# A hybrid decoder block on one core: the second projection unit of the first half in plain products instead of Strassen-Winograd products

## The chip, the cores and the metric

The kernel runs on one core of a Trainium2 chip. The metric is the device time of one execution in microseconds; the time of a kernel is the median of its runs. The core's engines work side by side, each on its own queue of instructions in a fixed order: TensorE (PE, matrix products into PSUM), VectorE (DVE), ScalarE (ACT), GpSimd (POOL), and SyncE (SP), which here issues all DMA transfers. An instruction that waits holds up what stands behind it on its engine.

## The reference

The block takes 2048 tokens of width 1024: a normalised input goes through one projection to two mixers (gated linear attention in chunks, and a short gated convolution), their outputs through one output projection, and then through a SwiGLU feed-forward part.

```python
h = rmsnorm(x, norm1_g[l])
proj = h @ w_in[l]
p_q, p_k, p_v, p_g, p_a, c_b, c_c, c_h = jnp.split(proj, splits, axis=-1)
...
log_a = (jax.nn.log_sigmoid(p_a @ w_gate_up[l] + b_gate[l]) / GATE_NORMALIZER)
o = gla_chunked(q, k, v, log_a)
o = rmsnorm(o, gla_norm_g[l]) * jax.nn.silu(p_g)
o_conv = c_b * causal_depthwise_conv(c_c * c_h, conv_w[l])
x = x + jnp.concatenate([o_gla, o_conv], axis=-1) @ w_out[l]
x = x + (jax.nn.silu(h2 @ w_ffn_gate[l]) * (h2 @ w_ffn_up[l])) @ w_ffn_down[l]
return rmsnorm(x, norm_f_g)
```

## The kernel before

**Precision.** Every float32 operand of a product is held as two parts, a high one that ACT rounds off and a low one that DVE gets by subtraction (`split`, L146 and L147). One step of a product (`product_step`, L334 to L336) is three matmuls of 128x128 by 128x512: high by high, high by low, low by high.

**Tiling.** Activations are transposed: features on the partitions, tokens along the row, in tiles of 128x512 (`h`). The 2048 tokens go in two halves of 1024, each half in two column blocks j = 0 and 1. The normalised input of a half is a 2x2 matrix of blocks B11 (features 0 to 511, j = 0), B12 (the same, j = 1), B21 and B22 (features 512 to 1023), each of four tiles k.

**Units.** The columns of a weight matrix are taken in units of 256, a 2x2 matrix of quarters A11, A12, A21, A22. `unit` computes a unit's four output tiles (r, j) with seven products instead of eight (the Winograd form of Strassen's method, `PRODUCTS`): A11 B11, S1 T1, S2 T2, A12 B21, S3 T3, S4 B22, A22 T4. The S are sums and differences of weight quarters, which POOL makes (L317, L318, L319, L324). The T are differences of activation blocks: T1 = B12 - B11, T2 = B22 - T1, T3 = B22 - B12, T4 = B21 - T2. A product is four steps, twelve matmuls. The outputs come out of sums of products: ACT copies a bank of PSUM (L354), PE adds a further product to the same bank, which must wait for the copy, and DVE adds the bank to a copy (L358). Split weights go into four buffers (`wq`), raw weights into two (`raw`), split activations (`op`) into 28.

**The first half's start.** `build_first` (L259) scales the tiles by the norm (DVE, L460), splits them, and computes unit 0 (the first 256 columns, the keys) beside that in eight plain products straight from the B blocks (L283 to L285), since the T don't exist yet. It then has POOL make the sixteen tiles of T1 to T4 (L294; each is written over one of the `h` tiles: T1, T2 and T4 over those of B11, T3 over those of B12) and splits them. Unit 1 (the queries) and all later units go through `unit` with the T. B12 itself has no further reader after unit 0, and its buffers go to later `op` tiles.

**Projections of a half.** `in_proj` (L556) takes twelve units: keys, queries, two of values, two of the output gate with silu (units 4 and 5), and six for the convolution. A step of other work is put in after each product (`tick`, L187): a list `background` of generators, of which one step is taken at every tick while `hurry` is set, later at every second. The list for the first half is `gate_weights`, a number of empty steps (`pause(6)`, L995), `row_stats(2)` and `row_stats(3)` (squares of the second half's rows on ACT, L412), `gate(0, ops)` (the forget gate: sixteen and twenty-four small-weight products into a_ps, L517, then exp, ln and scans, L538 to L551, and stores to s_d), and `h1_ahead`, the second half's B and T ahead of their use (L460, L240 to L253 and splits named hi and lo). The gate uses exp and ln, the output gate uses silu; ACT must load a table when it changes between them.

**Order.** The calls above give the program's order; a scheduler with its own time model then moves instructions on each engine's queue as dependencies allow. At run time each queue is taken in order.

Of the kernel before, what the change touches and what calls it, by code (L numbers as in the profile page):

```python
# [14 lines left out]
ALU = mybir.AluOpType  # L15
# [32 lines left out]
def tile_hymba_block(ctx, tc, x, xt, win, wa, wgu, wout, wffn, wdown, wdown_first, small, out):  # L48
# [149 lines left out]
    def pause(n):  # L198
        for _ in range(n):
            yield  # L200
# [6 lines left out]
    def split_op(src):  # L207
        o = opp.tile([P, 2, PB], F32R, name="op", tag="op")
        split(src, o[:, 0, :], o[:, 1, :])
        return o  # L210
# [48 lines left out]
    def build_first(quad, w):  # L259


        ops = {b: [] for _, b in PRODUCTS}
        h, o = {}, {}
        quarters = ("A11", "A12"), ("A21", "A22")
        los = []
        for j in range(2):
            for r in range(2):
                o[r, j] = bank()
            for k in range(KD):
                with ExitStack() as stack:  # L270
                    if len(los) > 1:
                        stack.enter_context(tc.issue_after(los[-2].ins))
                    h[k, j] = quad(k, j)
                x = opp.tile([P, 2, PB], F32R, name="op", tag="op")
                los.append(split(h[k, j][:], x[:, 0, :], x[:, 1, :]))
                if j == 0 and k >= PT:
                    row_squares(1, k - PT)
                name = ("B11", "B12")[j] if k < 4 else ("B21", "B22")[j]
                ops.setdefault(name, []).append(x)
                c = slice(k % 4 * P, (k % 4 + 1) * P)  # L280
                for r in range(2):
                    q = w[quarters[r][k // 4]]
                    pe.matmul(o[r, j][:], q[:, 0, c], x[:, 0, :], start=k == 0, stop=False)  # L283
                    pe.matmul(o[r, j][:], q[:, 0, c], x[:, 1, :], start=False, stop=False)
                    pe.matmul(o[r, j][:], q[:, 1, c], x[:, 0, :], start=False, stop=k == KD - 1)  # L285
            if j == 0:
                rbs[1] = rows_rstd(squares[1])
        for n, y, a, b in (
            ("T1", (0, 0), (0, 1), (0, 0)), ("T2", (0, 0), (4, 1), (0, 0)),
            ("T3", (0, 1), (4, 1), (0, 1)), ("T4", (0, 0), (4, 0), (0, 0)),  # L290
        ):
            for k in range(4):
                yy, aa, bb = [h[k + dk, j] for dk, j in (y, a, b)]
                pool.tensor_tensor(yy[:], aa[:], bb[:], ALU.subtract)  # L294
                ops[n].append(split_op(yy[:]))
        return ops, [(r, j, o[r, j], True) for j in range(2) for r in range(2)]

    def weight_quarter(src):
        n = src.shape[-1]
# [38 lines left out]
    def unit(src, ops, into=None):  # L338


        w = unit_weights(src)

        def mul(i, o=None):
            first = o is None
            o = bank() if first else o
            n, m = PRODUCTS[i]
            for k in range(len(ops[m])):
                product_step(o, w[n], ops[m], k, first)
            tick()
            return o  # L350

        def copied(name, o, at):
            t = tt(name) if into is None else into[at]
            act.activation(t[:], o[:], AF.Copy)  # L354
            return t

        def plus(t, o):
            dve.tensor_tensor(t[:], o[:], t[:], ALU.add)  # L358
            return t


        oa = mul(0)
        c11 = copied("c11", oa, (0, 0))
        ob = mul(1)
        c22 = copied("c22", ob, (1, 1))
        mul(2, oa)
        c12 = copied("c12", oa, (0, 1))
        plus(c11, mul(3))
        mul(4, oa)
        plus(c22, oa)  # L370
        mul(5, ob)
        plus(c12, ob)
        mul(6, oa)
        if into is not None:
            copied("c21", oa, (1, 0))
        return [(0, 0, c11, False), (1, 1, c22, False), (0, 1, c12, False), (1, 0, oa, True)]
# [176 lines left out]
            yield  # L553
        decays[b] = em, dn, el

    def in_proj(half, ops, first):  # L556
        def units():
            for u in range(12):
                with ExitStack() as stack:
                    if half == 0 and u == 1:  # L560
                        stack.enter_context(tc.issue_after(last_load[0].ins))
                    yield first if u == 0 and first else unit(win[u], ops)

        units = units()
        for dst, i0 in ((s_kq, 0), (s_kq, 2), (s_v, 0), (s_v, 2)):
            for r, j, c, p in next(units):
                store(dst[2 * half + j][i0 + r][:], settled(c, p)[:])
        for i0 in (0, 2):
            for r, j, c, p in next(units):
                store(s_g[2 * half + j][i0 + r][:], silu(c, p)[:])  # L570
        background.append(gla_half(half))
        for i0 in (0, 2):
            cc = {(r, j): settled(c, p) for r, j, c, p in next(units)}
            ch = {(r, j): c for r, j, c, _ in next(units)}
            for r in range(2):
                i = i0 + r
                for j in range(2):
                    s = tp.tile([P, PB + 2], F32, name="u", tag="t")
                    dve.tensor_tensor(s[:, 2:], ch[r, j][:], cc[r, j][:], ALU.mult)
                    dve.tensor_copy(s[:, 0:2], halo[:, i, :])  # L580
                    dve.tensor_copy(halo[:, i, :], s[:, PB : PB + 2])
                    y = cc[r, j]
                    dve.tensor_scalar(y[:], s[:, 0:PB], col(C_CW + i), None, ALU.mult)
                    for n in (1, 2):
                        dve.scalar_tensor_tensor(
                            y[:], s[:, n : n + PB], col(C_CW + 4 * n + i), y[:], ALU.mult, ALU.add
                        )
            for r, j, c, _ in next(units):
                y = cc[r, j]
                dve.tensor_tensor(y[:], c[:], y[:], ALU.mult)  # L590
                hi = tp.tile([P, PB], F32R, name="hi", tag="t")
                split(y[:], hi[:], y[:].bitcast(F32R))
                dst = s_mix[2 * half + j][i0 + r]
                store(dst[:, 0, :], hi[:].bitcast(F32))
                store(dst[:, 1, :], y[:])
# [338 lines left out]
    def last_unit(src, ops, b12, y, ssq):  # L934
# [49 lines left out]
        for j in range(2):  # L984
# [3 lines left out]
    act.preload_act_table_set("natural_log_exp_and_others")  # L988
    first_loads()
    load(wgu_sb[:], wgu)  # L990
    ops, first = build_h()
    hurry.append(True)
    background.extend(
        [
            gate_weights(), pause(6), row_stats(2), row_stats(3), gate(0, ops), unhurried(),  # L995
            h1_ahead(),
        ]
    )
    in_proj(0, ops, first)
    drain_background(lambda: len(background) < 2)  # L1000
    ops = load_pairs(s_h1)
    background.append(gate(1, ops))
    in_proj(1, ops, None)
    drain_background(lambda: (1, PT - 1) in done)
    ssq = out_proj(0, build_mix(0))
    drain_background(lambda: (3, PT - 1) in done)
# [117 lines left out]
```

## Time and profile before

| what | value |
| --- | --- |
| runs | 2144.77, 2137.0, 2141.64 us; median 2141.64 |
| profiled execution | 2147.18 us, its span 2145.4 us |
| PE busy | 2052.6 us, 96% of the span |
| DVE, ACT, POOL busy | 1438.1, 1008.4, 983.5 us |
| mean granted clock of PE | 0.983 |

The profile shows one execution. A page gives the busy time of each engine and the groups of instructions; the timeline gives instructions in order of time (start, duration, engine, line, operation, what is written and read, and in brackets the idle time before it and what ended that); the table of waits gives, for each pair of waiting and releasing line, the time in total, how often, and the longest. Matmul durations overlap, since one enters the array while the one before drains: what a matmul costs is the distance between two starts. Where a row shows an instruction many times (x6), its duration spans them all. Line numbers are those of the kernel before.

### The profile page before, as it was taken

What the parts mean: (1) busy time and instruction counts of PE and PEld (TensorE: products, weight loads), DVE (VectorE), ACT (ScalarE), POOL (GpSimd) and SP (SyncE); (2) the same over time, 40 slices, a digit from 0 to 9 for tenths busy, and PEclk for the clock granted to TensorE, in tenths of its full rate; (3) what the DMA queues carried; (4) which work ended last, traced back from release to release, by engine and by line L of the source; (5) the groups of instructions that cost most, each with busy time, mean ns of one, the idle gap of its engine ahead of it and who ended that gap; (6) DMA issues with size and microseconds to landing.
All of it is one profiled execution on the core that took longest, in us unless ns stands there. A gap on an engine that the chain in (4) does not pass through costs nothing.

```text
span 2145.4 us, 26958 instructions
## 1 busy us (share of the span) xinstructions
PE 2052.6 (96%) x9137; PEld 1658.6 (77%) x9137; DVE 1438.1 (67%) x2035; ACT 1008.4 (47%) x1961; POOL 983.5 (46%) x707
## 2 busy tenths in 40 slices
PE   6899899999999999999999999999999999999996
PEld 4677787887788887788888887787888888887774
DVE  7668975548664496688887674654686677664554
ACT  6455345564544334554555453333464454553344
POOL 3425422221201374555655436774644654435773
PEclk9899999999999999999999999999999999999998
DMA  7348667432486982466454577688455455587662
GB/s 270 125 145 296 225 267 249 154 121 88 154 305 190 348 295 103 167 246 220 181 226 177 208 303 266 257 333 351 155 199 210 148 188 196 186 334 275 265 265 108
DMA packets 191563, 471.85 MB, mean 220 GB/s; under 512 B 20032, under 2 KB 65344, under 8 KB 181824
## 3 DMA queue, kind: packets, MB, share of 16 engines
q1 hardware_dynamic: 191424, 470.12, 60.5%
q8 instruction: 72, 1.18, 0.2%
q14 instruction: 67, 0.55, 0.1%
HBM read 301.22 MB, written 168.82 MB: 219 GB/s over the span
## 4 chain that ended last, share of the span: by engine, by line
PE 73%; DMA 10%; DVE 10%; issue 3%; ACT 3%; POOL 1%; SPq 0%; DVEq 0%; ACTq 0%; POOLq 0%
PE mm L334 21%; PE mm L336 21%; PE mm L335 21%; DVE wq L147 2%; PE mm L742 2%; PE mm L745 2%; PE mm L743 2%; DMA raw<-in_wdown_dram 1%; DVE op L147 1%; DMA op<-sa_B 1%; DVE h L460 1%; DMA op<-shT 1%; DMA raw<-in_wffn_dram 1%; PE a_ps L517 1%; DVE so L147 1%
## 5 line engine op out<-in xcount | busy, mean ns | idle before, releaser
L334 PE MATMUL mm<-op,wq 128*128 128x512 f32 x2495 | 987.4, 398 | 31.1 <-ACT c L354 17.0
L336 PE MATMUL mm<-op,wq 128*128 128x512 f32 x2495 | 971.7, 394 | 19.6 <-DVE wq L147 18.8
L335 PE MATMUL mm<-op,wq 128*128 128x512 f32 x2495 | 979.0, 392 | 2.6 <-DVE op L147 2.6
L147 DVE TENSOR_TENSOR wq<-raw,wq 128x512 fp32r<-128x512 f32 (+2 forms) x628 | 532.2, 852 | 306.7 <-ACT wq L146 304.9
L146 ACT ACTIVATE wq<-raw 128x512 fp32r<-128x512 f32 (+2 forms) x628 | 367.7, 589 | 582.1 <-PE mm L336 416.0
L334 PEld LDWEIGHTS mm<-op,wq 128*128 128x128 f32 x2495 | 473.2, 190 | 151.2 <-ACT c L354 22.9
L336 PEld LDWEIGHTS mm<-op,wq 128*128 128x128 f32 x2495 | 473.1, 190 | 129.9 <-DVE wq L147 30.4
L335 PEld LDWEIGHTS mm<-op,wq 128*128 128x128 f32 x2495 | 473.9, 190 | 102.2 <-DVE op L147 4.3
L319 POOL TENSOR_TENSOR raw<-s,raw 128x512 f32<-128x512 f32 (+2 forms) x98 | 130.8, 1335 | 439.2 <-DVE wq L147 391.2
L358 DVE TENSOR_TENSOR c<-mm,c 128x512 f32<-128x512 f32 x270 | 185.3, 686 | 121.7 <-PE mm L336 119.6
L317 POOL TENSOR_TENSOR s<-raw 128x512 f32<-128x512 f32 (+2 forms) x98 | 128.5, 1311 | 196.5 <-DMA raw<-in_wffn_dram 92.2
L324 POOL TENSOR_TENSOR raw<-raw 128x512 f32<-128x512 f32 (+2 forms) x98 | 128.6, 1313 | 144.6 <-DVE wq L147 119.5
L354 ACT ACTIVATE c<-mm 128x512 f32<-128x512 f32 x270 | 156.6, 586 | 27.6 <-PE mm L336 27.0
L724 POOL TENSOR_TENSOR ssx<-ssx,q 128x512 f32<-128x512 f32 x52 | 74.6, 1447 | 152.8 <-ACT q L723 152.7
L318 POOL TENSOR_TENSOR raw<-raw 128x512 f32<-128x512 f32 (+2 forms) x98 | 138.5, 1414 | 4.5
L904 POOL TENSOR_TENSOR y<-c,y 128x512 f32<-128x512 f32 x66 | 99.3, 1506 | 68.4 <-DVE c L358 68.2
L146 ACT ACTIVATE wq<-s 128x512 fp32r<-128x512 f32 (+2 forms) x98 | 57.7, 589 | 103.3 <-PE mm L336 101.1
L147 DVE TENSOR_TENSOR so<-t,so 128x512 fp32r<-128x512 f32 x100 | 89.5, 902 | 23.5 <-ACT so L146 23.4
L742 PE MATMUL mm<-op,wq 128*128 128x512 f32 x256 | 100.7, 394 | 0.0
L743 PE MATMUL mm<-op,wq 128*128 128x512 f32 x256 | 99.8, 390 | 0.0
L147 DVE TENSOR_TENSOR wq<-s,wq 128x512 fp32r<-128x512 f32 (+2 forms) x98 | 87.0, 888 | 15.7 <-ACT wq L146 15.1
L146 ACT ACTIVATE so<-t 128x512 fp32r<-128x512 f32 x100 | 62.7, 629 | 48.4 <-DMA sa_B<-so 22.5
(173 smaller groups left out, 1893.1 us busy)
## 6 DMA issues: line engine op xcount, KB each, us to landing
raw<-in_wffn_dram SPq DMA_DIRECT2D x44, 1024.0 KB, 5.9
sa_T<-so SPq DMA_DIRECT2D x88, 512.0 KB, 4.6
op<-sa_T SPq DMA_DIRECT2D x88, 512.0 KB, 9.6
sa_B<-so SPq DMA_DIRECT2D x69, 512.0 KB, 3.4
op<-sa_B SPq DMA_DIRECT2D x69, 512.0 KB, 9.5
raw<-in_win_dram SPq DMA_DIRECT2D x23, 1024.0 KB, 5.7
raw<-in_wdown_dram SPq DMA_DIRECT2D x24, 768.0 KB, 6.2
sx<-y SPq DMA_DIRECT2D x48, 256.0 KB, 4.8
```

Source lines behind the costliest of these rows:

```text
L146: last_hi[:] = [act.activation(hi, src, AF.Copy)]
L147: return dve.tensor_tensor(lo, src, hi.bitcast(F32), ALU.subtract)
L318: pool.tensor_tensor(a21, a11, a21, ALU.subtract)
L319: pool.tensor_tensor(a11, s1, a11, ALU.subtract)
L324: pool.tensor_tensor(a12, a12, a11, ALU.subtract)
L334: pe.matmul(o[:], wh, xh, start=first and k == 0, stop=False, skip_group_check=True)
L335: pe.matmul(o[:], wh, xl, start=False, stop=False, skip_group_check=True)
L336: return pe.matmul(o[:], wl, xh, start=False, stop=k == n - 1, skip_group_check=True)
L354: act.activation(t[:], o[:], AF.Copy)
L358: dve.tensor_tensor(t[:], o[:], t[:], ALU.add)
L742: pe.matmul(o[e, j][:], wh, m[:, 0, :], start=k == 0, stop=False)
L743: pe.matmul(o[e, j][:], wh, m[:, 1, :], start=False, stop=False)
```

## The change

`build_first` no longer makes the differences itself but returns a function `differences(wanted)` that does. `plain_unit` computes a unit in eight plain products from the raw quarters and B11, B12, B21 and B22, 96 matmuls, with a tick after each. `in_proj` calls `differences` for T1, T2 and T3 ahead of unit 1, takes unit 1 of the first half through `plain_unit`, and calls it for T4 behind unit 1, when B12 is given up. The empty steps in `background` go from six to nine. The second half is as before.

```diff
-        for n, y, a, b in (
-            ("T1", (0, 0), (0, 1), (0, 0)), ("T2", (0, 0), (4, 1), (0, 0)),
-            ("T3", (0, 1), (4, 1), (0, 1)), ("T4", (0, 0), (4, 0), (0, 0)),
-        ):
-            for k in range(4):
-                yy, aa, bb = [h[k + dk, j] for dk, j in (y, a, b)]
-                pool.tensor_tensor(yy[:], aa[:], bb[:], ALU.subtract)
-                ops[n].append(split_op(yy[:]))
-        return ops, [(r, j, o[r, j], True) for j in range(2) for r in range(2)]
+
+        def differences(wanted):
+            for n, y, a, b in (
+                ("T1", (0, 0), (0, 1), (0, 0)), ("T2", (0, 0), (4, 1), (0, 0)),
+                ("T3", (0, 1), (4, 1), (0, 1)), ("T4", (0, 0), (4, 0), (0, 0)),
+            ):
+                for k in range(4 if n in wanted else 0):
+                    yy, aa, bb = [h[k + dk, j] for dk, j in (y, a, b)]
+                    pool.tensor_tensor(yy[:], aa[:], bb[:], ALU.subtract)
+                    ops[n].append(split_op(yy[:]))
+
+        return ops, [(r, j, o[r, j], True) for j in range(2) for r in range(2)], differences
+
+    def plain_unit(src, ops):
+
+        raw = raw_weights(src)
+        us, columns = [], (("B11", "B21"), ("B12", "B22"))
+        for r, row in enumerate(((0, 1), (3, 2))):
+            w = [weight_quarter(raw[:, i, :]) for i in row]
+            for j in range(2):
+                o = bank()
+                for i, n in enumerate(columns[j]):
+                    for k in range(4):
+                        product_step(o, w[i], ops[n], k, i == 0)
+                    tick()
+                us.append((r, j, settled(o, True), False))
+        return us
...
-    def in_proj(half, ops, first):
+    def in_proj(half, ops, first=None, differences=None):
...
-                    yield first if u == 0 and first else unit(win[u], ops)
+                    if half or u > 1:
+                        us = unit(win[u], ops)
+                    else:
+                        us = plain_unit(win[u], ops) if u else first
+                if half == 0 and u == 1:
+                    del ops["B12"]
+                    differences(("T4",))
+                yield us
 
         units = units()
+        if half == 0:
+            differences(("T1", "T2", "T3"))
...
-            gate_weights(), pause(6), row_stats(2), row_stats(3), gate(0, ops), unhurried(),
+            gate_weights(), pause(9), row_stats(2), row_stats(3), gate(0, ops), unhurried(),
```

More of the change, by code (lines that the diff above doesn't have):

```diff
@@ L990, in tile_hymba_block @@
     load(wgu_sb[:], wgu)
-    ops, first = build_h()
+    ops, first, differences = build_h()
     hurry.append(True)
@@ L998, in tile_hymba_block @@
     )
-    in_proj(0, ops, first)
+    in_proj(0, ops, first, differences)
     drain_background(lambda: len(background) < 2)
@@ L1002, in tile_hymba_block @@
     background.append(gate(1, ops))
-    in_proj(1, ops, None)
+    in_proj(1, ops)
     drain_background(lambda: (1, PT - 1) in done)
```

## The prediction, made before the changed kernel ran

> **What bounds the kernel now.** The page first: TensorE (PE) is busy for nearly the whole span, so what can be won lies where PE waits or runs at a low clock.
>
> ```profile
> span 2145.4 us, 26958 instructions
> PE 2052.6 (96%) x9137; PEld 1658.6 (77%) x9137; DVE 1438.1 (67%) x2035; ACT 1008.4 (47%) x1961; POOL 983.5 (46%) x707
> ```
>
> Then the busy time by stretches (columns: bounds, length, PE, weight loads, DVE, ACT, POOL, granted clock, DMA share, GB/s). In the first stretch below PE finishes unit 1, the unit that is changed; the second is unit 2.
>
> ```profile
> 52.43:90.09 37.66, 27.99 (x96) 20.76 (x95) 29.52 (x34) 14.23 (x27) 22.68 (x15) 0.82 0.17 63
> 90.09:109.60 19.51, 19.51 (x89) 16.07 (x88) 7.09 (x12) 11.91 (x28) 5.19 (x4) 1.00 0.69 242
> 150.00:262.00 112.00, 100.57 (x419) 79.95 (x418) 105.19 (x132) 53.90 (x96) 60.02 (x36) 0.97 0.79 263
> ```
>
> Unit 2 issues 89 matmuls in 19.5 us, the stretch before it 96 in 37.7 us. PE's waits between 30 and 91 us, longest sum first, say for what:
>
> ```profile
> PE mm L336 <- DVE wq L147: 7.5, 3, 3.6
> PE mm L335 <- DVE op L147: 2.6, 4, 1.1
> ```
>
> DVE makes the low parts of weights (wq) and operands (op), both at L147, and PE takes them as they come. The PE rows give the rest of the price:
>
> ```profile
> 52.43 0.40 PE L285 MATMUL mm<-op,wq 128*128 128x512 f32 x1
> 60.87 0.79 PE L336 MATMUL mm<-op,wq 128*128 128x512 f32 x1 [3.47 <-DVE wq L147]
> 74.74 0.79 PE L336 MATMUL mm<-op,wq 128*128 128x512 f32 x1 [3.63 <-DVE wq L147]
> 75.33 0.63 PE L334 MATMUL mm<-op,wq 128*128 128x512 f32 x1
> 79.17 0.61 PE L334 MATMUL mm<-op,wq 128*128 128x512 f32 x1
> 82.16 0.39 PE L334 MATMUL mm<-op,wq 128*128 128x512 f32 x1
> 86.24 0.39 PE L334 MATMUL mm<-op,wq 128*128 128x512 f32 x1
> 89.87 0.62 PE L336 MATMUL mm<-op,wq 128*128 128x512 f32 x2
> ```
>
> From 82.16 to 86.24 lie 18 matmuls: 0.227 us each. From 75.33 to 79.17, behind the stall of 3.63, lie nine: 0.427 us each. So a stall of this length costs about ten slow matmuls more, 10 x 0.20 = 2.0 us. By the order of the built program 24 matmuls of unit 2 stand ahead of the last of unit 1, which is in the row of 89.87. At 90.32 PE has thus done unit 1 and 24 of unit 2; without them unit 1 ends at 90.32 - 24 x 0.227 = **84.9**. This is the mark to compare with.
>
> **Part 1: unit 1.** It has 84 matmuls (seven products of twelve), with operands T1 to T4 and combined weights; the plain unit has 96, with the four B operands and raw quarters alone. Added on PE: 12 x 0.227 = 2.7 us. Removed: three weight splits on ACT and DVE, three additions on DVE, four combinations on POOL. What PE waits for now follows from DVE's queue, which runs without a gap:
>
> ```profile
> 45.33 1.13 DVE L147 TENSOR_TENSOR wq<-raw,wq 128x512 fp32r<-128x512 f32 x1
> 46.38 1.78 DVE L147 TENSOR_TENSOR wq<-s,wq 128x512 fp32r<-128x512 f32 x1
> 48.08 8.08 DVE L147 TENSOR_TENSOR op<-h,op 128x512 fp32r<-128x512 f32 x6
> 56.08 1.24 DVE L414 TENSOR_TENSOR ssq<-ssq 128x4 f32<-128x4 f32 x1
> 57.36 1.19 DVE L422 TENSOR_SCALAR msq<-ssq 128x4 f32<-128x4 f32 x1
> 62.43 2.37 DVE L147 TENSOR_TENSOR op<-h,op 128x512 fp32r<-128x512 f32 x2
> 64.72 1.24 DVE L156 TENSOR_TENSOR rl<-ry 128x4 f32<-128x4 f32 x1
> 67.14 0.68 DVE L147 TENSOR_TENSOR op<-h,op 128x512 fp32r<-128x512 f32 x1
> 74.01 1.28 DVE L147 TENSOR_TENSOR wq<-raw,wq 128x512 fp32r<-128x512 f32 x2
> ```
>
> A split takes 0.64 us alone (74.01: two in 1.28) and 1.2 to 1.35 while POOL works (62.43, 48.08); even a 128x4 operation takes 1.24. POOL's own pace:
>
> ```profile
> 33.01 2.97 POOL L294 TENSOR_TENSOR h<-h 128x512 f32<-128x512 f32 x2 [31.20 <-DVE h L460]
> ...
> 42.46 6.86 POOL L294 TENSOR_TENSOR h<-h 128x512 f32<-128x512 f32 x4
> 49.27 1.74 POOL L319 TENSOR_TENSOR raw<-s,raw 128x512 f32<-128x512 f32 x1
> 52.24 3.37 POOL L294 TENSOR_TENSOR h<-h 128x512 f32<-128x512 f32 x2 [1.23 <-DVE op L147]
> ```
>
> 1.7 us each under contention. The order of the changed program puts the splits of A11 and A12 (unit 1's first row of quarters) where A11 and S1 stand now, and A21 behind: six op, ssq, msq, two op, rl, one op, rl, msq. Up to 48.1 nothing differs. POOL's first ten (T1, T3 and two combinations of unit 2) are done at about 33 + 10 x 1.7 = 50; T2 then waits for T1's splits, since it is written over it. So of the six op the first takes 1.35, two run partly free (1.05 and 0.65): T1[0] is split at 51.1, and T2 starts. Three more at 1.35: 55.2. ssq and msq 2.4: 57.6. Two op 2.4: 60.0. rl 1.2, op 1.2, rl 1.2: 63.6. T2 ends at 51.1 + 4 x 1.7 = 57.9 and T4[0..2] follow from 58.8, 60.5, 62.4, so POOL works until 64.1; msq ends at 64.2, and A21's low part stands at **64.9**.
>
> PE meanwhile: 24 matmuls of unit 1 stand between those of unit 0 (13 now), so unit 0 ends 11 x 0.227 = 2.5 us behind 52.4 at the latest, at 54.9 or sooner. 24 more of the first row need only what is there: 60.4 at the latest; four with A21's high part: 61.3 (ACT has it by 58.1, behind T2[2], which POOL ends at 51.1 + 3 x 1.7 = 56.2, and three steps of 0.63). Then PE waits until 65.0, some four us, and runs slow for a while. Left are 96 - 24 - 24 - 4 = 44: 65.0 + 44 x 0.227 + 2.0 = **77.0**. Against 84.9 the front wins **7.9 us**.
>
> Bounds. With every DVE operation at the contended pace (1.35 a split, 1.2 a small one: nine splits, five small ones and A21's own behind 48.1), A21 comes at 48.1 + 10 x 1.35 + 5 x 1.2 = 67.6, and the gain is 5.2. With none after 50, A21 is there at 56 to 57, PE never waits, and unit 1 ends at 54.9 + 72 x 0.227 = 71.2: 13.7. I take 7.9, since most of the stretch keeps POOL at work as in the rows of before.
>
> The Trainium skill, "TensorE: Matmul & The Clock Gate", Part 1, says that the clock halves after an idle window of about 3.4 us; rows 60.87 and 74.74 (3.47 and 3.63 idle, then 0.427 us a matmul) agree. By it a remaining wait under that length would save the 2.0 us, and the sum would come to 9.9.
>
> What the change lays on others here costs nothing: T4's four splits need the buffers of B12, which PE frees with the last product but one of unit 1 (the last of them 12 matmuls ahead of 77.0, at 74.3), and behind them on ACT queue a copy and unit 2's S2. S2 is needed 24 matmuls into unit 2, 5.4 us behind 77.0, and four splits at 0.63 are over before. Without that cover each would cost PE its 0.64. Unit 2's A11 and S1 stand on DVE behind A22 and five op, eight splits behind 64.9: by 73. Unit 1's four stores and one load on SP stay.
>
> **Part 2: the gate's place.** pause goes from 6 to 9 and unit 1 gives 8 ticks for 7, so the gate of the forget path comes two ticks later, into units 4 and 5. There silu starts, and the two need different activation tables: the order of the changed program has 10 table loads between unit 4 and the recurrence, now 2 (the rows of 154.44 and 193.51), and 3 more in the second half.
>
> ```profile
> 149.08 0.58 ACT L354 ACTIVATE c<-mm 128x512 f32<-128x512 f32 x1
> 154.44 1.28 ACT L390 ACT_TABLE_LOAD   x1
> 155.74 0.63 ACT L390 ACTIVATE c<-c 128x512 f32<-128x512 f32 x1
> 169.91 1.08 ACT L354 ACTIVATE c<-mm 128x512 f32<-128x512 f32 x2
> 170.56 0.51 PE L334 MATMUL mm<-op,wq 128*128 128x512 f32 x1 [3.04 <-ACT c L354]
> 193.51 1.28 ACT L601 ACT_TABLE_LOAD   x1
> ```
>
> The critical place is ACT between unit 4's third copy (149.08) and unit 5's first (169.91): PE must have the latter before it adds to that bank. PE's work between is 84 matmuls and two small ones, 19.5 us. ACT takes 20.8 now, with one load and some ten us in which it waits for DVE, and PE waits 3.04. Changed, 27 instructions stand there, seven of them loads; with the stretch's mean of 53.90/96 = 0.56 for the others, 7 x 1.28 + 20 x 0.56 = 20.2. Bounds: all of ACT's waits stay and six loads come on top, +7.7; or the loads fill the waits and today's 3.04 with its slow matmuls goes, -4. I take **+1**: only two splits of the look-ahead for the second half, which are what ACT waits for, stand there, against six now, but DVE stays as full (105.19 of 112). In the second half the loads cost 0 to 3 x 1.28 = 3.9; I take 0:
>
> ```profile
> 425.74 1.28 ACT L390 ACT_TABLE_LOAD   x1
> ...
> 461.29 1.28 ACT L601 ACT_TABLE_LOAD   x1
> ```
>
> ```profile
> 400.00:450.00 50.00, 50.00 (x279) 40.89 (x278) 26.12 (x58) 34.91 (x83) 11.01 (x8) 1.00 0.44 143
> 450.00:500.00 50.00, 50.00 (x230) 39.60 (x229) 28.72 (x56) 27.60 (x56) 10.72 (x8) 1.00 0.30 95
> ```
>
> Seven loads stand there now, the first and the last shown, and PE has no gap beside them. The gate also brings its four stores of s_d to SP two ticks later, past unit 4's stores and the look-ahead's loads, and SP stands still until DVE has each:
>
> ```profile
> SPq L141 <- DVE g L549: 16.0, 4, 9.0
> ```
>
> Behind them wait loads of raw weights, issued a unit (19.5 us) before their use; 9.0 us more are covered by that, and without it would come out whole. The readers of s_d come only with the recurrence.
>
> The Trainium skill, "ScalarE: Activation LUTs", What ACT_TABLE_LOAD costs, adds a drain of about 1.38 us to each load; row 155.74 begins 1.30 behind the load's start, so no drain shows here. By the page the six extra loads of the critical place would be an estimated 16.0 us of ACT, where the upper bound above has 7.7.
>
> **Sum.** -7.9 + 1 + 0 = -6.9. The profiled execution took 2147.2 us (span 2145.4 and 1.8 around it), so 2140.3; the median of the runs lies 5.5 lower, 2141.6, which gives **2134.7**.
>
> **The rivals.**
> *The loads eat the gain.* The ping-pong of tables delays unit 5's and 6's copies by 3 to 6 us: 2137 to 2141, no change to be told. For it: 20.2 us of ACT against 19.5 of PE leaves no room. Against it: ACT idles for half of 150 to 262 (53.90 of 112).
> *Slower.* The loads hold up ACT's weight splits, DVE starves behind them, and the look-ahead moves into the convolution units. It needs both the upper bound of the loads (+7.7, and 3.9 in the second half) and three more stalls past 3 us with 2.0 us of slow clock each: -5.2 + 11.6 + 6 = +12.4, 2154. It decides from the point where units 4 to 11 lose more than the front wins, 8 us. For it: DVE has 7 us of slack in 112.
> *The front doesn't give it.* DVE, not the differences, sets unit 1: if A21 comes at 69 or later (the copies and squares on ACT ahead of its high part), the gain is under 4: 2138 to 2142.
> *More.* POOL is quiet early and PE never waits: 13.7 and today's stall at 170 gone: 2126.
>
> **Chances.** Forecast (2131 to 2136) 0.45, more 0.07, loads eat it 0.21, front fails 0.10, slower 0.17. 0.3% of 2141.6 is 6.4 us, about what a measurement of this kernel can tell from no change. Faster 0.52, same 0.31, slower 0.17. Range: from the large gain to the foot of the slower case, 2126 to 2147; the forecast's own is 2128 to 2139.
>
> **What will show it.** Unit 1's 96 matmuls end near 77; one PE wait of three to five us on a weight's low part near 61 to 65, against two now; DVE's fifth weight split of the differences' stretch near 65; unit 2 without a gap. At units 4 and 5, ten table loads, and PE's wait for the copy under 4 us. Wrong, if a wait for a first copy grows past 6, or unit 1 ends behind 81.

## The result and the profile after

| | before | after |
| --- | --- | --- |
| median of 16 runs each | 2140.57 us | 2147.05 us |
| lowest to highest | 2132.22 to 2144.77 us | 2142.31 to 2150.92 us |
| ratio, 95% interval | | 1.0031, 1.0022 to 1.0041 |
| profiled execution, its span | 2147.18, 2145.4 us | 2145.19, 2143.1 us |

The change made the kernel 0.31% slower, some 6.6 us. The two profiled executions stand the other way round: that of before lies 6.6 us above its median, that of after 1.9 us below. So spans of single executions are not compared here; stages are, and ratios.

The page of the changed kernel begins (span; busy time of each engine):

```profile
span 2143.1 us, 26967 instructions
PE 2050.9 (96%) x9149; PEld 1655.2 (77%) x9149; DVE 1437.0 (67%) x2029; ACT 1018.3 (48%) x1969; POOL 975.8 (46%) x703
```

PE has its twelve matmuls more (9149 for 9137), ACT ten microseconds more. Now the stretches, of before and then of after (length, PE, weight loads, DVE, ACT, POOL, granted clock, DMA share, GB/s):

```profile
30.00:91.00 61.00, 47.97 (x169) 34.67 (x168) 50.16 (x56) 29.88 (x63) 40.86 (x26) 0.86 0.30 112
110.00:150.00 40.00, 39.52 (x164) 29.41 (x163) 23.83 (x53) 21.25 (x44) 5.17 (x4) 1.00 0.34 120
150.00:200.00 50.00, 45.50 (x190) 36.17 (x189) 45.86 (x51) 27.77 (x48) 29.75 (x18) 0.97 0.86 291
200.00:270.00 70.00, 63.08 (x266) 50.40 (x265) 63.33 (x87) 28.51 (x52) 34.15 (x21) 0.98 0.68 227
```

```profile
30.00:91.00 61.00, 54.32 (x224) 41.88 (x223) 46.51 (x56) 31.74 (x67) 35.70 (x23) 0.97 0.41 141
110.00:150.00 40.00, 37.32 (x150) 26.90 (x150) 21.36 (x44) 20.63 (x41) 6.47 (x5) 1.00 0.38 138
150.00:200.00 50.00, 43.62 (x176) 34.60 (x176) 42.75 (x51) 36.24 (x57) 24.92 (x16) 0.93 0.68 227
200.00:270.00 70.00, 58.50 (x231) 44.11 (x230) 64.53 (x87) 27.95 (x52) 30.98 (x20) 0.95 0.75 247
```

By the counts of matmuls the front is ahead: 224 against 169 until 91 us, 55 more, of which twelve are the plain unit's own. The other 43 are 43 x 0.227 = 9.8 us of work done sooner. Then it is given back, and more: 14 matmuls fewer from 110 to 150, 14 from 150 to 200 and 35 from 200 to 270, 63 x 0.227 = 14.3 us. (A few records are missing from any trace, so such counts are good to a microsecond or two.)

The changed unit itself, by the stores of keys and queries (first to last issue), before and after:

```profile
L141 SPq DMA_DIRECT2D sk<-c x5: 319/320/327, 59.9 to 90.9; - x5
```

```profile
L141 SPq DMA_DIRECT2D sk<-c x6: 319/354/910, 60.9 to 77.9; - x6
```

Unit 1's last output is on its way at 77.9, 13.0 us earlier. In the kernel before, 24 matmuls of unit 2 stood ahead of it, 5.4 us, so the front won 7.6 us.

What PE waits for from 110 to 270 us (units 4 to 8), before and after (sum, how often, longest):

```profile
PE mm L334 <- ACT c L354: 8.0, 5, 3.0
PE mm L336 <- DVE wq L147: 3.3, 3, 1.8
```

```profile
PE mm L354 <- DVE wq L147: 11.5, 7, 4.9
PE mm L352 <- ACT c L372: 5.1, 5, 2.4
```

With the smaller ones of the same view the waits rise from 11.8 to 20.5 us, and their kind changes. The copies of banks, which the prediction had its eye on, cost less than before (5.1 for 8.0). The low parts of weights on DVE cost 11.5 for 3.3. The longest of them, in the timeline of after, first ACT (start, duration, what is done, idle before it):

```profile
147.55 1.28 ACT L408 ACT_TABLE_LOAD   x1
148.84 0.63 ACT L408 ACTIVATE c<-c 128x512 f32<-128x512 f32 x1
149.49 1.28 ACT L558 ACT_TABLE_LOAD   x1
...
151.53 1.28 ACT L559 ACT_TABLE_LOAD   x1
152.83 0.72 ACT L559 ACTIVATE g<-g,ones 128x512 f32<-128x512 f32 x1
...
154.08 1.28 ACT L568 ACT_TABLE_LOAD   x1
...
156.13 1.28 ACT L408 ACT_TABLE_LOAD   x1
```

then DVE, then PE:

```profile
153.58 0.69 DVE L560 TENSOR_TENSOR g<-g,g 128x512 f32<-128x512 f32 x1 [3.26 <-ACT g L559]
...
157.31 1.29 DVE L569 TENSOR_TENSOR dn<-em,el 128x4 f32<-128x4 f32 x1
158.52 3.45 DVE L563 TENSOR_TENSOR_SCAN g<-ones,g 128x128 f32<-128x128 f32 x4
161.90 0.66 DVE L147 TENSOR_TENSOR wq<-raw,wq 128x512 fp32r<-128x512 f32 x1
...
163.75 1.75 DVE L147 TENSOR_TENSOR wq<-raw,wq 128x512 fp32r<-128x512 f32 x1
```

```profile
160.25 0.39 PE L353 MATMUL mm<-op,wq 128*128 128x512 f32 x1
165.55 0.80 PE L354 MATMUL mm<-op,wq 128*128 128x512 f32 x1 [4.91 <-DVE wq L147]
166.14 0.63 PE L352 MATMUL mm<-op,wq 128*128 128x512 f32 x1
...
171.26 0.57 PE L352 MATMUL mm<-op,wq 128*128 128x512 f32 x1
```

ACT spends 6.4 us of its time from 147.55 to 157.41 on five table loads. The gate's step at L560 on DVE needs ACT's L559, and DVE, which takes its queue in order, stands 3.26 us in front of it. What it must do after that comes late in a bunch: the scans, which take 3.45 us here, and then the weights' low parts. PE stands from 160.25 to 165.55 and then runs at half rate until 171.26 (0.427 us from start to start). DVE's waits for the gate's steps on ACT over the whole stretch of 110 to 270 us, in the table of waits of after:

```profile
DVE g L557 <- ACT g L556: 6.6, 2, 3.9
...
DVE g L560 <- ACT g L559: 4.6, 3, 3.3
```

These are 11.2 us, for 2.3 before (1.6 at L539, 0.7 at L542). Not all of them lie where DVE is full. The two of L557 end at 124.94 us (3.90) and 143.55 (2.69), and of those of L560 only the 3.26 us of row 153.58 lie behind 150. From 110 to 150 us DVE is busy for 21.36 of 40.00 us, so it had time to spare there; such a wait takes little, but puts off what stands behind it. The look-ahead, which follows the gate, begins with its first scaled tile at 154.79 us (146.76 before, 138.07 in run 1 below). A larger wait of DVE, that for the high parts of weights from ACT, does not go with the time: it is 15.2 us for 11.7 before, but 19.2 in run 10, one of the fastest.

### The profile page after: what moved, and what is told of

Read it like the earlier page. It is cut to its first block, busy times and chain, and to the rows that moved or that the text cites. A ratio compares the mean times of both kernels' runs of the same rounds, so it can differ in the third digit from the quotient of the medians.

```text
span 2143.1 us, 26967 instructions
## 1 busy us (share of the span) xinstructions
PE 2050.9 (96%) x9149; PEld 1655.2 (77%) x9149; DVE 1437.0 (67%) x2029; ACT 1018.3 (48%) x1969; POOL 975.8 (46%) x703
## 4 chain that ended last, share of the span: by engine, by line
PE 69%; DMA 9%; DVE 7%; ACT 2%; issue 2%; POOL 1%; SPq 0%; DVEq 0%; ACTq 0%; POOLq 0%
PE mm L352 19%; PE mm L354 19%; PE mm L353 19%; PE mm L769 3%; PE mm L772 3%; PE mm L770 3%; DMA raw<-in_wdown_dram 2%; DVE wq L147 2%; DVE so L147 1%; DMA raw<-in_wffn_dram 1%; DMA op<-sa_T 1%; DMA op<-sa_B 1%; DMA op<-shT 1%; DMA shT<-so 1%; DVE h L478 1%
## 5 line engine op out<-in xcount | busy, mean ns | idle before, releaser
L147 DVE TENSOR_TENSOR wq<-raw,wq 128x512 fp32r<-128x512 f32 (+2 forms) x626 | 526.9, 847 | 313.2 <-ACT wq L146 308.1
L342 POOL TENSOR_TENSOR raw<-raw 128x512 f32<-128x512 f32 (+2 forms) x97 | 125.5, 1293 | 129.9 <-DVE wq L147 114.0
L336 POOL TENSOR_TENSOR raw<-raw 128x512 f32<-128x512 f32 (+2 forms) x97 | 136.7, 1410 | 4.5
L147 DVE TENSOR_TENSOR wq<-s,wq 128x512 fp32r<-128x512 f32 (+2 forms) x97 | 82.4, 850 | 17.5 <-ACT wq L146 17.0
```

Of the source, the lines that this page charges most:

```text
L147: return dve.tensor_tensor(lo, src, hi.bitcast(F32), ALU.subtract)
L336: pool.tensor_tensor(a21, a11, a21, ALU.subtract)
```

## The experiments

Each kernel was timed in alternation with the kernel before; a ratio under 1 is faster than before. Runs 3 and 5 to 7 leave out the silu of the first half's output gate, so they time a kernel that computes something else. "Early" and "late" are the gate's place, set by the number of empty steps. In the kernel before, six steps put it into the quiet stretch ahead of the silu; with the plain unit, which gives one tick more, six or seven do the same, and the change has nine. The last column is DVE's busy time of the 70.00 us from 200 to 270.

| kernel | gate | table loads, 90 to 300 us | ratio, 95% interval | PE waits, 110 to 270 us | DVE busy, 200 to 270 us |
| --- | --- | --- | --- | --- | --- |
| before | early | 2 | 1 | 11.8 | 63.33 |
| after | late | 10 | 1.0031, 1.0022 to 1.0041 | 20.5 | 64.53 |
| 1 plain unit, seven empty steps | early | 2 | 0.9972, 0.9961 to 0.9983 | 12.0 | 55.92 |
| 2 kernel before, eight empty steps | late | 10 | 1.0073, 1.0059 to 1.0087 | 17.9 | 69.85 |
| 3 after, no silu in the first half | late | 0 | 1.0007, 0.9998 to 1.0017 | 18.5 | 60.69 |
| 4 kernel before, two empty steps behind the gate | early | 2 | 0.9993, 0.9983 to 1.0003 | 11.2 | 64.01 |
| 5 kernel before, no silu in the first half | early | 0 | 1.0007, 0.9996 to 1.0017 | 13.9 | 64.47 |
| 6 seven empty steps, no silu | early | 0 | 0.9986, 0.9976 to 0.9996 | 14.6 | 57.73 |
| 7 kernel before, eight steps, no silu | late | 0 | 1.0057, 1.0042 to 1.0072 | 15.8 | 68.14 |
| 8 as 1, more loads | early | 15 | 1.0006, 0.9996 to 1.0015 | 18.1 | 62.55 |
| 9 as 1, look-ahead later | early | 2 | 0.9963, 0.9948 to 0.9977 | 11.8 | 59.48 |
| 10 plain unit, six empty steps | early | 2 | 0.9963, 0.9950 to 0.9976 | 11.3 | 57.85 |
| 11 after, look-ahead later | late | 10 | 1.0053, 1.0033 to 1.0073 | 23.4 | 69.47 |
| 12 as 10, look-ahead later | early | 2 | 0.9962, 0.9948 to 0.9976 | 12.4 | 55.77 |

**1. The plain unit with the gate back in its place.** The late gate is undone, the rest of the change stays.

```diff
-            gate_weights(), pause(9), row_stats(2), row_stats(3), gate(0, ops), unhurried(),
+            gate_weights(), pause(7), row_stats(2), row_stats(3), gate(0, ops), unhurried(),
```

> The changed kernel with seven empty steps instead of nine, which puts the forget gate back to where it stands against unit 2 in the kernel before; 2 table loads between unit 4 and the recurrence instead of 10. Theory (the gate's later place costs what the front wins): ratio to before 0.994 to 0.998, the front's gain of some 8 us kept. Rival (the plain unit itself or the new order behind it loses it): 1.001 to 1.005, as the changed kernel.

2137.46 us against 2142.3: faster than both kernels. The front's gain is thus real and is left in the end time, and what the change lost, it lost by two empty steps: 1.0031 - 0.9972 = 0.0059, or 12.6 us (give or take 0.0014, 3 us). PE's waits from 110 to 270 us are again those of the kernel before:

```profile
PE mm L352 <- ACT c L372: 7.7, 5, 3.4
PE mm L354 <- DVE wq L147: 3.6, 3, 2.0
```

**2. The late gate alone, without the plain unit.**

```diff
-            gate_weights(), pause(6), row_stats(2), row_stats(3), gate(0, ops), unhurried(),
+            gate_weights(), pause(8), row_stats(2), row_stats(3), gate(0, ops), unhurried(),
```

> The kernel before with eight empty steps instead of six: unit 1 in Strassen products, the gate two ticks later as in the changed kernel, 10 table loads instead of 2. Theory: slower by what the changed kernel lost behind its front, 10 to 15 us, ratio 1.004 to 1.007. Rival (the plain unit is what costs): 0.999 to 1.002.

2157.83 us, ratio 1.0073: 15.6 us by the late gate alone. So the price isn't one of the plain unit's, and the two halves of the change add up within their intervals.

**3. The change without its table loads.** The first half's silu becomes a plain copy and the load ahead of the recurrence is left out, so that no table changes there; the gate stays late.

```diff
-                store(s_g[2 * half + j][i0 + r][:], silu(c, p)[:])
+                store(s_g[2 * half + j][i0 + r][:], (silu if half else settled)(c, p)[:])
...
```

> The changed kernel with a plain copy in place of silu in the first half, so that no table load is left there while the gate stays at its later place. Left out: silu of the output gate in the first half. If the table loads are what costs: ratio to before 0.993 to 0.997. If the gate's later place costs by itself (its work on ACT and DVE beside the look-ahead): 1.000 to 1.004.

2143.95 us, ratio 1.0007, 0.0024 less than the change with its ten loads: 5 us. But it is still 0.0035 above run 1, so the loads are not all of it. The waits say the same, low parts above all:

```profile
PE mm L352 <- ACT c L372: 7.3, 4, 2.8
PE mm L354 <- DVE wq L147: 7.2, 6, 3.3
```

**4. Two empty steps behind the gate, in the kernel before,** meant to move the look-ahead for the second half on, alone.

```diff
-            gate_weights(), pause(6), row_stats(2), row_stats(3), gate(0, ops), unhurried(),
+            gate_weights(), pause(6), row_stats(2), row_stats(3), gate(0, ops), pause(2), unhurried(),
```

> The kernel before with two empty steps behind the gate, so that the look-ahead for the second half alone starts two ticks later, and the gate stays. If the look-ahead's shift towards the convolution units is what costs: 1.003 to 1.006. If it is the gate or its table loads: 0.999 to 1.002.

2140.07 us, ratio 0.9993 (0.9983 to 1.0003). This run decides nothing: in its trace the look-ahead's scaled tiles stand on DVE from 147.3 to 222.2 us, in that of before from 146.8 to 222.6. The scheduler had moved them up again. Runs 9 and 11 repeat the question by other means.

**5, 6 and 7. The early and the late gate, all without silu in the first half.** The edit of run 3, applied to the kernel before (5), to the plain unit with seven empty steps (6), and to the kernel before with eight (7).

> The kernel before with a copy in place of silu in the first half: no table load there, the gate in its place. Left out: silu of the output gate in the first half. The mark for the two runs without silu that follow. Two loads go, both beside other work: 0.998 to 1.001 by either theory.

> The changed kernel with seven empty steps and a copy in place of silu in the first half. Left out: silu of the output gate in the first half. Beside the changed kernel without silu (gate late, ratio 1.0007) it shows what the late gate costs without any table load. If the place costs by itself: 0.996 to 0.998, so 6 to 10 us of place. If all that the late gate costs is table loads: 0.999 to 1.002, the same as with the gate late.

> The kernel before with eight empty steps and a copy in place of silu in the first half. Left out: silu of the output gate in the first half. With silu the late gate cost this kernel 15 us (1.0073). If that is the table loads: 0.999 to 1.002. If it is the place as such: 1.004 to 1.008. Half of each: 1.003.

2142.62, 2139.86 and 2154.75 us. Without any load the late gate costs 1.0007 - 0.9986 = 0.0021 with the plain unit (4.5 us) and 1.0057 - 1.0007 = 0.0050 without it (10.7 us), each give or take some 0.0015 (3 us). With silu it was 12.6 and 15.6 us. By this the loads have 8 and 5 us of the price, with 4 to 5 us of uncertainty, and the place the rest. The subtraction isn't clean: leaving out silu should only save time, but run 6 is 0.0014 slower than run 1, with intervals that overlap, and its 0.9986 lies between the two ranges expected.

**8. Table loads without a late gate.** Run 1, with the silu table loaded behind each of the four logarithms of the first half's gate, so that the tables change back and forth at the early place: 15 loads from 90 to 300 us for 2.

```diff
-            act.activation(t1[:], t1[:], AF.Ln, bias=one_t)
+            ln = act.activation(t1[:], t1[:], AF.Ln, bias=one_t)
+            if b < 2:
+                with tc.issue_after(ln.ins):
+                    act.preload_act_table_set("silu_and_others")
```

> The changed kernel with seven empty steps, and the silu table loaded behind each of the first half's four ln steps of the gate, which brings 14 table loads into the first half instead of 2 while the gate stays at its place. If a load costs PE its 1.28 us there: 12 more loads, 15 us, ratio 1.004. If the loads fill ACT's waits: 0.997 to 0.999, as without them (0.9972).

2142.9 us, ratio 1.0006, 0.0034 above run 1: 7.3 us for 13 loads, 0.56 us each, not quite half of the 1.28 that a load takes on ACT. PE's waits rise from 12.0 to 18.1 us. On DVE the gate begins where it did, at 122.58 us (121.59 in run 1), but the loads put its end off, from 148.5 to 159.1 us, and DVE waits for its steps on ACT for 8.0 us (1.6). So here too ACT's lateness reaches DVE through the gate. At this price the change's eight additional loads make 4.5 us, as run 3 has it (5 us). So the loads alone cost time, and that time isn't all of the 12.6.

**9. The look-ahead later, alone.** Run 1 with one constraint: the look-ahead's first scaled tile is issued behind a weight split of unit 5.

```diff
-            return scaled(col(g + k), rb[j], h)
+            with ExitStack() as stack:
+                if g == C_G1 and 4 * k + 2 * j < 1:
+                    stack.enter_context(tc.issue_after(wq_los[-4].ins))
+                return scaled(col(g + k), rb[j], h)
...
-            gate_weights(), pause(7), row_stats(2), row_stats(3), gate(0, ops), unhurried(),
+            gate_weights(), pause(7), row_stats(2), row_stats(3), gate(0, ops), pause(3), unhurried(),
```

> The changed kernel with seven empty steps (the gate early, two table loads in the first half, as in the best run so far, ratio 0.9972), and the look-ahead for the second half alone moved back: its first scaled tile is issued behind a weight split of unit 5, so that from the third tile on the scaled tiles stand between the same weight splits on DVE as in the changed kernel (the third behind 33 of them, the twelfth behind 49, the last behind 55; with the look-ahead unmoved 28, 45 and 51). Theory A, the late gate costs because it pushes the look-ahead on, past the place where DVE has room: the 4.5 us that the place cost without any loads come back, ratio 0.9985 to 1.0005, and PE's waits for low parts of weights between 150 and 270 us grow by 3 us or more. Theory B, the gate itself and its loads are all of the price and the look-ahead is free to stand here or there: within 2 us of the run with the early gate, ratio 0.9963 to 0.9982.

2132.7 us against 2140.46, ratio 0.9963. The look-ahead did move: its last scaled tile begins at 225.3 us (213.0 in run 1), its last low part ends at 238.4 (228.9). It costs nothing, so theory A falls for a shift of some 10 us. In the changed kernel, where the same tile stands behind about as many weight splits, it begins later still, at 238.3 us; so late a look-ahead with an early gate was not run. PE's waits in sum don't change; they are only of another kind, more for low parts and fewer for copies:

```profile
PE mm L357 <- DVE wq L147: 6.2, 7, 2.3
PE mm L355 <- ACT c L375: 4.9, 4, 2.4
```

**10. The gate one tick earlier still.**

```diff
-            gate_weights(), pause(9), row_stats(2), row_stats(3), gate(0, ops), unhurried(),
+            gate_weights(), pause(6), row_stats(2), row_stats(3), gate(0, ops), unhurried(),
```

> The changed kernel with six empty steps, as the kernel before has, so that the gate comes one tick earlier still than in the run with seven; two table loads in the first half. If the price of the gate's place falls steadily with each tick (some 6 us a tick from nine to seven), ratio 0.995 or less. If the price was that of meeting unit 5 and the silu, it is already gone with seven: 0.9963 to 0.9982. If the gate now meets the front, where DVE has no room until the differences are split, it is slower than with seven: 0.999 or more.

2131.73 us, ratio 0.9963, within the interval of run 1. So the price doesn't grow by so much a tick: it is that of meeting units 4 and 5, and is gone once the gate is ahead of them. This is the simplest edit of those with the lowest ratios, and beats both kernels: 0.37% (0.24 to 0.50) under the kernel before.

**11. The look-ahead moved out of the late gate's way.** The constraint of run 9 in the changed kernel, on a split that is later still, with nine empty steps ahead of the gate and two behind it.

> The changed kernel with its nine empty steps, its late gate and its ten table loads in the first half, and only the look-ahead for the second half moved back, out of the gate's way: from the third on its scaled tiles stand behind 36, 38, 39, 40, 43 weight splits on DVE and the last behind 56, where the changed kernel has 32, 33, 35, 37, 40 and 55. Theory A, what the late gate costs beside its loads is that it meets the look-ahead (the four scans take 3.45 us beside it and 1.36 alone, and low parts of weights wait behind them): the 4.5 us that the place cost without loads come back, ratio 0.9985 to 1.0018, PE's worst wait for a low part at 160 us falls from 4.9 to under 3.5, and the late gate ends before 167 us (170.2 in the changed kernel). Theory B, the loads and the gate's own work in units 4 and 5 are the whole price: 1.0022 to 1.0041, as the changed kernel.

2152.81 us against 2143.7, ratio 1.0053. In the place itself theory A was met: the late gate ends at 166.1 us for 170.2, and no wait for a low part exceeds 2.85 us. But the time did not come back as theory A had it (0.9985 to 1.0018), and it lies above theory B's range too, though its interval overlaps that of the change. The stretches of this kernel:

```profile
150.00:200.00 50.00, 41.88 (x164) 32.08 (x163) 36.16 (x46) 34.52 (x54) 22.45 (x15) 0.93 0.64 221
200.00:270.00 70.00, 58.00 (x228) 44.43 (x227) 69.47 (x90) 28.37 (x51) 34.34 (x21) 0.93 0.71 242
```

From 150 to 200 us DVE does 36.16 us of work, 6.6 less than in the changed kernel (42.75) and 9.7 less than before (45.86). DVE's waits for the gate's steps on ACT (6.6 and 4.6 us) are those of the changed kernel, so this work was moved by the edit and not by the gate. It has to be done from 200 to 270 us, where DVE is now busy for 69.47 of 70.00 us, and every weight's low part stands in that queue. A look-ahead this late may thus have a price, which run 9 could not show.

The last column of the table goes with the ratio over all kernels. DVE is busy for 55.77 to 59.48 us in the five fastest (runs 1, 6, 9, 10 and 12), which have the plain unit and the early gate, for 62.55 to 64.53 in the kernel before, runs 4, 5 and 8 and the change, and for 68.14 to 69.85 in the three slowest (runs 2, 7 and 11), all with the late gate; run 3 has 60.69. This is a ranking and not a test, and the kernels with the plain unit are some 8 us ahead in their work. It fits a price that is paid late: what DVE hasn't done by 200 us, it does in a stretch with little or no room for it. How much of that is due to DVE's waits, how much to the gate's own work and how much to the look-ahead, these runs do not separate. Nor do they settle the share of the slow scans: they take 2.42 us in this run, so they were not alone here either.

**12. Both edits that gave 0.9963.** Six empty steps, and the look-ahead tied as in run 9, to a split that suits this order.

> The changed kernel with six empty steps (the gate two ticks earlier, two table loads in the first half; 0.9963 alone) and the look-ahead's first scaled tile issued behind a weight split of unit 5 (the third tile then behind 29, the fourth behind 32 weight splits, where it was 28 and 28). Both edits gave 0.9963 each. If what they save is the same waits between 110 and 270 us, it stays at 0.995 to 0.997; if they save different ones, 0.993 to 0.9945; if the look-ahead now ends too late for the convolution units, 0.998 or more.

2134.42 us against 2143.7, ratio 0.9962: they save the same, not two things. With the gate early there is little left to win there by moving work about; PE waits 11.3 to 12.4 us in all of these.

What remains open: the place's price without loads is 4.5 us with the plain unit and 10.7 without it, a difference of 0.0029 with some 0.0023 of uncertainty. The traces have one thing that would fit it: from 150 to 262 us DVE does 4.6 us of work on the gate's tiles in run 3 and 9.9 in run 7, whose gate comes some 8 us later. That was not tested. Nor was the gate moved late with the look-ahead kept early: the look-ahead follows the gate in the kernel's order, and that was not tried.

## Why the prediction was wrong, step by step

**Part 1, the front: right.** Predicted were 7.9 us (5.2 to 13.7). By the stores it is 7.6, by the ratios of runs 10 and 1, which have the plain unit and the early gate, 0.0037 and 0.0028 of 2141 us: 7.9 and 6.0. One wait on a weight's low part is left, as said, between 61 and 65 us:

```profile
62.20 0.40 PE L353 MATMUL mm<-op,wq 128*128 128x512 f32 x1
65.35 0.50 PE L354 MATMUL mm<-op,wq 128*128 128x512 f32 x1 [2.75 <-DVE wq L147]
...
66.03 0.63 PE L353 MATMUL mm<-op,wq 128*128 128x512 f32 x1
...
69.01 0.49 PE L354 MATMUL mm<-op,wq 128*128 128x512 f32 x1
```

A21's low part was forecast for 64.9; the row of DVE (64.62, 0.68 long) has it at 65.3:

```profile
49.92 7.00 DVE L147 TENSOR_TENSOR op<-h,op 128x512 fp32r<-128x512 f32 x6
...
59.26 1.28 DVE L147 TENSOR_TENSOR op<-h,op 128x512 fp32r<-128x512 f32 x2
...
64.62 0.68 DVE L147 TENSOR_TENSOR wq<-raw,wq 128x512 fp32r<-128x512 f32 x1
```

The wait came out at 2.75 us instead of some four, and the slow matmuls behind it (seven steps of 0.427 from 66.03 to 69.01) at 1.4 us for 2.0. The working from DVE's queue ended within half a microsecond, in part by luck. The six op splits began at 49.92 us instead of 48.08, and the three that follow took 0.64 to 0.68 us each, the price of a split alone, instead of 1.2: 1.8 us too late and 1.6 too quick cancel. The twelve more matmuls and the moved splits of T4 cost no more than was said; unit 2 shows no gap.

**Part 2, the gate's place: this step failed.** The prediction put "I take +1" on it, between -4 and +7.7. On the chip it cost 12.6 us against run 1 and 14.5 against run 10 (1.0031 - 0.9963 = 0.0068), above the upper bound. The ten table loads were there. What failed is the sum for ACT, "27 instructions stand there, seven of them loads", 20.2 us against PE's 19.5. The trace has these 27 and the seven loads between the two copies, but in 26.4 us:

```profile
140.04 0.58 ACT L372 ACTIVATE c<-mm 128x512 f32<-128x512 f32 x1
...
162.05 1.28 ACT L566 ACT_TABLE_LOAD   x1 [2.43 <-DVE g L563]
...
166.40 0.59 ACT L372 ACTIVATE c<-mm 128x512 f32<-128x512 f32 x1
```

ACT works for 20.5 us of that, as summed. For 5.9 it waits, 3.5 for PE and 2.4 for the gate's scans on DVE, and the sum behind the +1 had these waits at nothing: the gate goes from ACT to DVE and back, and the loads come in between. The price was also looked for at the wrong wait. PE's waits for copies shrank (8.0 to 5.1), as the lower bound had it, while those for DVE's low parts rose (3.3 to 11.5). And the sum had a term for this one place alone: of the 63 matmuls given back, 35 go behind it, from 200 to 270 us, for which it had none. The row that the step quoted for DVE, 105.19 of 112.00 us, was the one to work from. In these 112 us DVE now does 5.1 us of work on the gate's tiles, for 0.7 before, and stands for 3.3 us in front of the gate's step on ACT, where it had 7 us of room. The bound, taken from ACT alone, couldn't hold that. Of the 12.6 us, runs 3, 6 and 8 give some 5 to 8 to the loads and the rest to the place; how the rest divides further stays open.

None of the signs named beforehand for being wrong appeared: no wait for a copy grew past 2.44 us, and unit 1 was done by 77.9. They watched the copies, and the price came by the low parts.

**The second half's loads: right.** They were taken at nothing, with 3.9 as the bound. Ten loads stand there now, from 429 to 469 us, and PE has one wait of 0.7 us from 400 to 500 us; run 1 has the same loads and the same wait. The kernel before has none there, so "nothing" was right to within 0.7 us.

**The stores of s_d: right.** From 90 to 300 us SP waits for them for 8.9 us, 4.7 at the longest (16.0 and 9.0 before), and no wait of PE for a raw weight follows.

**The rivals.** "Slower" had 0.17 and came nearest. It decides, as it says, "from the point where units 4 to 11 lose more than the front wins, 8 us". Of its chain, "The loads hold up ACT's weight splits, DVE starves behind them", only the outline held: ACT is late and DVE passes it on to PE. But DVE's wait for ACT's weight splits does not go with the time (19.2 us in run 10, at 0.9963), while its waits for the gate's steps do: 7.5 to 11.2 us in the change and in runs 2, 3, 7, 8 and 11, 1.5 to 2.3 in all others. That the look-ahead moves on costs nothing by 12 us (run 9) and perhaps something by more (run 11). It took the upper bound of the loads and three long stalls to be needed; with the late gate's place beside the loads it needs less. "The loads eat the gain" was half right: 5 to 8 of the 12.6 us are theirs, but alone they would have left a result near no change, as run 8 shows (1.0006).

By what was measured, -7.9 for the front and +14.5 for the gate's place make +6.6 us; since both are differences from run 10, they must. Two figures that do not share a run, the front by its stores (-7.6) and the late gate alone in the kernel before (+15.6, run 2), make +8.0, with an uncertainty of some 3 us.

## What to carry to other kernels

Where a change moves work past its neighbours, price it on every in-order queue that it enters, and first on the one with the least room: here DVE had 7 us of room in 112, and the gate brought 4 us of work and 3 us of waiting into them. A change of two parts is best timed in two parts; here one line, the number of empty steps, turned a gain of 0.37% into a loss of 0.31%. And before a run with an edit to the order is read, its trace must show that the order has changed.

## What the hardware showed

**A table load held ACT for 1.28 to 1.30 us.** Behind the row of 147.55 the next activation begins at 148.84, behind that of 151.53 at 152.83: 1.29 and 1.30 from start to start. The Trainium skill, "ScalarE: Activation LUTs", What ACT_TABLE_LOAD costs, adds a drain of about 1.38 us to each; these rows show none. What a load costs the kernel is another number: 0.56 us each in run 8.

**A short wait can halve PE's clock, and a longer one need not.** Behind 2.75 us of idle time (the rows of 65.35 to 69.01 above) PE ran at half rate; the granted clock from 66 to 70 us is 0.60. In run 11 it stood longer and did not; the granted clock from 227 to 231 us is 1.00:

```profile
223.94 0.39 PE L356 MATMUL mm<-op,wq 128*128 128x512 f32 x1
227.17 0.50 PE L357 MATMUL mm<-op,wq 128*128 128x512 f32 x1 [2.85 <-DVE wq L147]
227.51 0.39 PE L355 MATMUL mm<-op,wq 128*128 128x512 f32 x1
227.74 0.40 PE L356 MATMUL mm<-op,wq 128*128 128x512 f32 x1
```

0.23 us from start to start at once. In run 8 even a wait of 3.58 us, up to 230.59, is followed by steps of 0.24 us at a clock of 1.00. In the changed kernel a wait of 2.44 us was followed by seven steps of 0.42 to 0.60 us, too, at a clock of 0.50 from 264 to 267 us:

```profile
264.03 0.80 PE L352 MATMUL mm<-op,wq 128*128 128x512 f32 x1 [2.44 <-ACT c L372]
...
266.76 0.59 PE L352 MATMUL mm<-op,wq 128*128 128x512 f32 x1
```

The Trainium skill, "TensorE: Matmul & The Clock Gate", Part 1, gives one idle window of about 3.4 us for the halving, a window that runs freely. That the same length of wait goes both ways would fit a free-running window, but halving behind 2.4 and 2.75 us doesn't fit the length. What one wait costs varies as well: in the front of all nine kernels with the plain unit PE waits for 2.73 to 2.75 us, and 5 to 13 slow steps follow. The prediction's side remark, that a wait below 3.4 us would save the slow matmuls, thus did not hold. The trace of the kernel before had a row against it already: behind a wait of 1.80 us, up to 226.22, eight steps of 0.42 to 0.45 us follow.

**Four scans take 3.45 us beside POOL's work and 1.37 alone.** POOL is busy for 2.88 of the 3.50 us from 158.5 in the changed kernel, with one tile of the look-ahead and one of the weights. The same line in the early place of run 1, where POOL stands from 138.8 to 140.2:

```profile
138.73 0.16 DVE L569 TENSOR_TENSOR dn<-em,el 128x4 f32<-128x4 f32 x1
138.81 1.37 DVE L563 TENSOR_TENSOR_SCAN g<-ones,g 128x128 f32<-128x128 f32 x4
```

and the 128x4 operation ahead of it 0.16 there and 1.29 in the changed kernel. In run 11 the scans took 2.42 us and no time came back; what the 2.1 us are worth alone was not tested.
